# One more piece of weight sums ahead of mixing, two weight chunks rounded at other places, and half of a scaling given to ScalarE

## The chip, the cores and the metric

The kernel runs on one core of a Trainium2 chip. The metric is the device time of one execution in microseconds. The core has five engines with instruction queues of their own: PE (matrix products), DVE (vector), ACT (scalar), POOL (GpSimd) and SP, which only issues transfers. Each runs its queue in order; semaphores tie them together.

## The reference

One decoder block for 512 positions of width 1024, all in float32. Cut to what matters here:

```python
h = rmsnorm(x, norm1_g)
z = h @ w_in + b_in                       # split in five: GLU, two for the recurrence, two gates
u = silu(layernorm(depthwise_conv31(glu(z))))
y_a = u @ conv_w_out + conv_b_out
y_b = (rg_lru(conv4(z_rx)) * gelu(z_rg)) @ lru_w_out
m = sigmoid(z_ga) * y_a + sigmoid(z_gb) * y_b
x = x + m @ w_mix_out                     # "mixing"
h = rmsnorm(x, norm2_g)                   # "norm 2"
x = x + (silu(h @ ffn_w1) * (h @ ffn_w3)) @ ffn_w2     # SwiGLU, width 2816
return rmsnorm(x, norm_f_g)
```

## The kernel before, in words

**Products in split float32.** Every float32 operand is split into a high part, rounded by a copy on ACT (`split_to`, L133: "cast"), and a low part, the difference, by a subtraction on DVE or POOL (L129). A product is three matmuls: high by high, high by low, low by high.

**Weight chunks.** Weights come in chunks of 128 x 1024, listed in the order of use. `emit_chunk` loads one into one of 4 raw buffers and rounds it into one of 5 split buffers (`hl`). `weights(key, ahead)` emits all chunks up to the one asked for and `ahead` more; the default look-ahead is 4. `emit_to(n)` emits chunks up to number n at the place where it stands in the code. At the end of mixing the chunks are, in order: `t2_2` and `t2_3` of mixing, then for SwiGLU `b11_1`, `b21_1`, `b11_2`, `b21_2`, `t4_1`, `t4_2`, `f1_0`, `f3_0`, `f1_1`, `f3_1`, and those for k=3. The profile shows the SwiGLU ones as `hl_fb`, `hl_ft` and `hl_f`. The low parts of `t4_2` and `f1_0` are POOL's, the others DVE's.

**Seven products instead of eight.** Mixing, most of SwiGLU's first two products and its last one use a scheme of two by two blocks in which sums of blocks are multiplied, seven products instead of eight. The sums of the weights' blocks are made by the kernel: a "piece" is two loads of 256 KB, four additions or subtractions, and a store of 512 KB to memory, from where the chunks are read later. `make_f_sums` does most pieces before mixing, one step of it after each matrix product; from step `SUMS_EACH[0]` to `SUMS_EACH[1]` a piece starts at each step, otherwise at every second or third. `OUT_IN` of the pieces for the last product are made there. `mix_end` makes three more, and `out_step` makes the rest during SwiGLU, where `OUT_PIECES` says in which of the steps of block k a piece begins (its loads are issued by POOL, its sums are DVE's). Three buffers hold the pieces (`wsums`).

**The end of mixing and norm 2.** Here the order on PE, ACT and DVE is written out by hand (`manual_schedule`); elsewhere a scheduler orders each engine's queue. `run` takes the last chunk of mixing with `get(kh - 1, ...)` and calls `mix_end`. There `second()` does the last products, six `plus` add them on DVE to four halves of the row tiles 0 and 1 of x (`x` at L940), and `scaled(t, 1)` does the rest of norm 2 for tiles t=0 and 1: the square of the second half on ACT (L561), the root on ACT (L562), the reciprocal on DVE (L563), and the scaling of both halves i=0, 1 into `xs` on DVE (L1100). Then PE does `third` for k=0 and 1, and `turn_half` turns the scaled tiles: for each of 8 columns c, PE transposes tiles 0 and 1 into a PSUM bank (`th`, L579), ACT rounds the high part (`h2<c>h`, L582), DVE makes the low part (`h2<c>l`, L583), after which the bank is free. It is called for c=0 to 3 and c=4 to 7 with six products of `third` behind each, and has four banks to go round. Columns 0 to 3 read half 0 of `xs`, columns 4 to 7 read half 1.

**Behind it** come the first halves of SwiGLU blocks 1 and 2 (`b0.half`, `b1.half`, `fourth`), with the turning of row tiles 2 and 3 between them (`turn`), also by hand and with two banks; then `b.first`, `f_inputs`, and block 0, which is not of the seven-product form and takes the chunks `f1_0`, `f3_0`, `f1_1`, `f3_1`.

Of the kernel before, what the change touches and what calls it, by code (L numbers as in the profile page):

```python
# [10 lines left out]
AF = mybir.ActivationFunctionType  # L11
ALU = mybir.AluOpType
# [22 lines left out]
AHEAD = 4  # L35
# [10 lines left out]
PIECES = 3  # L46


OUT_PIECES = {0: "1", 1: "101", 2: "01", 3: "11", 4: "101", 5: "101", 6: "101", 7: "111", 8: "101", 9: "101", 10: "100"}
SEVEN = (1, 2, 3, 4, 5, 6, 7, 8, 9, 10)  # L50


BEGUN, BEGUN_LATER = (1, 2), (3,)
SUMS_AT, SUMS_STEP, SUMS_LAG, STORE_LAG = 4, 3, 2, 5
SUMS_DENSE, SUMS_OWN, SUMS_EACH = 20, 52, (60, 68)


F_MIX, OUT_MIX, LATE_LAG = 2, 1, 8
OUT_IN = 1

KEPT = {2: 1, 3: 2, 4: 3, 5: 4, 6: 5, 7: 6, 8: 7, 9: 7, 10: 7}

# [34 lines left out]
def tile_block(ctx, tc, a, out):  # L97
# [25 lines left out]
    vec, act, pe, pool_e = nc.vector, nc.scalar, nc.tensor, nc.gpsimd  # L123


    newest = {}
# [19 lines left out]
    emitted = [0]  # L146
# [35 lines left out]
    def emit_to(n):  # L182
        while emitted[0] < min(len(chunks), n):
            emit_chunk()
# [67 lines left out]
    class Quartered:  # L252
# [39 lines left out]
        def get(self, k, *names, ahead=AHEAD):  # L292

            out = []
            for n in names:
                if n in self.parts:
                    out.append(self.parts[n][k])
                    continue
                key, i = self.at[n, k]
                if key not in self.loaded:  # L300
                    self.loaded[key] = weights(key, ahead)
                h, l = self.loaded[key]
                out.append((h[:, i, :], l[:, i, :]))
            return out
# [645 lines left out]
    class Sevenfold:  # L950
# [42 lines left out]
        def run(self, sums, begun, end):  # L993
# [4 lines left out]
            n, kh, get = self.name, self.kh, self.q.get  # L998
# [45 lines left out]
                        plus(2 + i, 1, r5[i])  # L1044

            act.activation(warm, late[-1][1][0][:, :1].bitcast(F32), AF.Sqrt, scale=0.0, bias=eps_t)
            last = get(kh - 1, "b22", "t2", "t3", ahead=AHEAD - 1)
            end(lambda: second(kh - 1, *last), plus, r1, r2, r7, third)

    m7 = Sevenfold(mixq)  # L1050
# [15 lines left out]
    x2 = [[longt(f"x2{t}{h}") for h in range(2)] for t in range(NT)]  # L1066
# [13 lines left out]
    def mix_end(second, plus, r1, r2, r7, third):  # L1080
        made = []

        def store():
            with tc.issue_after(newest["any"]):
                piece_store(*made.pop(0))

        for n in range(F_MIX + OUT_MIX):
            name, halves, dest = mix_todo.pop(0)
            with tc.issue_after(newest["any"]):
                made.append((piece_load(name, halves), dest))  # L1090
            if n < 2:
                piece_sums(*made[-1], pool_e)
        sc = [[longt(f"xs{t}{h}") for h in range(2)] for t in range(NT)]
        xs.extend(sc)
        begun = [rstd_begin(x2[t][0], sc[t][0]) for t in range(2)]

        def scaled(t, h):
            r = rstd_end(begun[t], x2[t][h], sc[t][h])
            for i in range(2):
                newest["scaled"] = vec.tensor_scalar(out=sc[t][i], in0=x2[t][i], scalar1=r, scalar2=None, op0=ALU.mult).ins  # L1100
                nc.sync.dma_start(x2_kept[t][i][:, :], x2[t][i])


        with tc.manual_schedule(engines={ET.PE, ET.Activation, ET.DVE}):
            second()
            plus(0, 1, r1[0])
            plus(0, 1, r2[0])
            plus(2, 1, r1[0])
            plus(1, 1, r1[1])
            plus(1, 1, r2[1])  # L1110
            plus(3, 1, r1[1])
            for t in range(2):
                scaled(t, 1)

            for i in range(2):
                third(i, range(2))
            for q in range(2):
                turn_half("th", xs, "norm2_g", h2p, 0, [bank, bank2], range(4 * q, 4 * q + 4))
                for i in range(2):
                    third(i, [2 + q])  # L1120


            for c in range(ND):
                f_full.append(longt(f"hf{c}"))
                full(f_full[c][:, LO], c, LO)
            with tc.issue_after(newest["full"]):
                piece_sums(*made[2], pool_e)
            for i in range(2):
                plus(2 + i, 1, r7[i])
                plus(2 + i, 0, r7[i])  # L1130
            begun.extend(rstd_begin(x2[t][1], sc[t][1]) for t in (2, 3))
            emit_to(emitted[0] + 1)
            for i in range(2):
                plus(2 + i, 0, r1[i])
            for t in (2, 3):
                scaled(t, 0)
        while made:
            store()

    m7.run(x2, lambda k: None, mix_end)  # L1140


    o7 = Sevenfold(outq, LATE_LAG)
    out_stores, out_n = [], [0]
    out_at, out_steps = [None, None], {k: list(v) for k, v in OUT_PIECES.items()}

# [150 lines left out]
    with tc.manual_schedule(engines={ET.PE, ET.Activation, ET.DVE}):  # L1297
# [20 lines left out]
        for b in (b0, b1):  # L1318
            b.copy()
            b.fourth_end()  # L1320
    with tc.issue_after(turned[0]), tc.issue_after(turned[1]):
        for b in begun.values():
            b.first()
        emit_to(emitted[0] + 4)
        f_inputs()

    for k in range(KF):
# [28 lines left out]
    x2 = [[longt(f"x2b{t}{h}") for h in range(2)] for t in range(NT)]  # L1356
# [99 lines left out]
```

## Time and profile before

| | |
|---|---|
| Median of 3 runs | 799.51 us (798.9 to 799.93) |
| The profiled execution | 798.86 us, span of its instructions 797.0 us |
| PE busy | 786.5 us (99%) |
| DVE busy | 695.8 us (87%) |
| ACT busy | 472.6 us (59%) |
| POOL busy | 360.2 us (45%) |
| Granted TensorE clock | 0.998 |

The profile comes from one execution. In its rows, `out<-in` are the kernel's tiles, `L` is the line of the kernel before, and a bracket says how long the engine was idle before and what ended that. In the rows of stages stand: the stretch in us, its length, busy time and instructions of PE, of its weight loads (PEld), of DVE, ACT and POOL, the clock, the share of the transfer engines, and GB/s. In the rows of time stand start and duration.

### The profile page before, as it was taken

What the parts mean: (1) busy time and instruction counts of PE and PEld (TensorE: products, weight loads), DVE (VectorE), ACT (ScalarE), POOL (GpSimd) and SP (SyncE); (2) the same over time, 40 slices, a digit from 0 to 9 for tenths busy, and PEclk for the clock granted to TensorE, in tenths of its full rate; (3) what the DMA queues carried; (4) which work ended last, traced back from release to release, by engine and by line L of the source; (5) the groups of instructions that cost most, each with busy time, mean ns of one, the idle gap of its engine ahead of it and who ended that gap; (6) DMA issues with size and microseconds to landing.
All of it is one profiled execution on the core that took longest, in us unless ns stands there. A gap on an engine that the chain in (4) does not pass through costs nothing.

```text
span 797.0 us, 12582 instructions
## 1 busy us (share of the span) xinstructions
PE 786.5 (99%) x4374; PEld 688.8 (86%) x4374; DVE 695.8 (87%) x1097; ACT 472.6 (59%) x674; POOL 360.2 (45%) x347
## 2 busy tenths in 40 slices
PE   8999999999999999999999999999999999999996
PEld 7988888888888888888888797999999999888885
DVE  5799999999998997985899868898877798999956
ACT  7446688777679665562326466544455555556843
POOL 2576778788869988853350482113222221000000
PEclk9999999999999999999999999999999999999999
DMA  7746566577776786979987987588998898878652
GB/s 222 190 122 177 157 191 201 174 236 236 195 246 212 249 264 195 295 236 295 296 293 240 275 259 217 157 267 269 343 309 291 297 325 299 235 235 269 197 169 105
DMA packets 181074, 188.13 MB, mean 236 GB/s; under 512 B 14119, under 2 KB 142035, under 8 KB 181011
## 3 DMA queue, kind: packets, MB, share of 16 engines
q1 hardware_dynamic: 172195, 156.66, 63.8%
q0 software_dynamic: 8672, 30.41, 11.2%
q8 instruction: 34, 0.56, 0.3%
q10 hardware_dynamic: 144, 0.26, 0.1%
q14 instruction: 29, 0.24, 0.1%
HBM read 145.48 MB, written 38.80 MB: 231 GB/s over the span
## 4 chain that ended last, share of the span: by engine, by line
PE 95%; DVE 2%; ACT 1%; DMA 0%; issue 0%; SPq 0%; DVEq 0%
PE z L539 35%; PE fr L1211 24%; PE or L991 13%; PE yb L539 7%; PE ya L539 5%; PE mxr L991 4%; PE g L860 3%; PE f L539 2%; PE fr L1255 1%; DMA x<-in_x_dram 0%; DVE x L940 0%; PE z L632 0%; PE th L579 0%; PE tx L590 0%; DVE xs L1100 0%
## 5 line engine op out<-in xcount | busy, mean ns | idle before, releaser
L733 DVE SCALAR_TENSOR_TENSOR cv<-u,par,cv 128x511 f32<-128x511 f32 (+17 forms) x240 | 162.6, 728 | 1.1 <-ACT cv L730 0.9
L129 POOL TENSOR_TENSOR hl_in<-raw_in,hl_in 128x1024 fp32r<-128x1024 f32 x51 | 123.3, 2422 | 64.2 <-ACT hl_in L133 43.4
L129 POOL TENSOR_TENSOR fws<-fws 128x256 f32<-128x256 f32 x120 | 104.7, 875 | 75.1 <-DMA fws<-in_ffn_w_dram 69.5
L398 POOL DMA_DIRECT2D ot<-fwso x21 | 15.3, 731 | 166.1 <-DVE fwso L129 158.8
L1211 PE MATMUL fr<-hs_0h,hl_ft 128*128 128x256 f32 x320 | 59.2, 283 | 0.0
L133 ACT CAST hl_in<-raw_in 128x1024 fp32r<-128x1024 f32 x51 | 53.1, 1043 | 2.2 <-DMA raw_in<-in_w_in_dram 1.0
L129 DVE TENSOR_TENSOR hl_ft<-raw_ft,hl_ft 128x1024 fp32r<-128x1024 f32 x39 | 47.5, 1219 | 4.7 <-ACT hl_ft L133 4.7
L129 DVE TENSOR_TENSOR hl_fb<-raw_fb,hl_fb 128x1024 fp32r<-128x1024 f32 x30 | 36.9, 1231 | 15.9 <-ACT hl_fb L133 15.9
L1211 PEld LDWEIGHTS fr<-hs_0h,hl_ft 128*128 128x128 f32 x320 | 50.6, 192 | 0.0
L133 ACT CAST hl_ft<-raw_ft 128x1024 fp32r<-128x1024 f32 x40 | 41.6, 1047 | 12.4 <-PE fr L1211 9.2
L133 ACT CAST hl_fb<-raw_fb 128x1024 fp32r<-128x1024 f32 x30 | 31.5, 1050 | 24.4 <-PE fr L1211 11.6
L1211 PE MATMUL fr<-hs_0l,hl_ft 128*128 128x256 f32 x160 | 45.3, 283 | 0.0
L539 PE MATMUL z<-h10h,hl_in 128*128 128x512 f32 (+1 forms) x110 | 41.4, 378 | 0.0
L539 PE MATMUL z<-h11h,hl_in 128*128 128x512 f32 (+1 forms) x110 | 41.1, 376 | 0.0
L539 PE MATMUL z<-h17h,hl_in 128*128 128x512 f32 (+1 forms) x110 | 41.1, 376 | 0.0
L539 PE MATMUL z<-h13h,hl_in 128*128 128x512 f32 (+1 forms) x110 | 41.1, 376 | 0.0
L539 PE MATMUL z<-h14h,hl_in 128*128 128x512 f32 (+1 forms) x110 | 41.1, 376 | 0.0
L539 PE MATMUL z<-h15h,hl_in 128*128 128x512 f32 (+1 forms) x110 | 41.1, 376 | 0.0
L539 PE MATMUL z<-h16h,hl_in 128*128 128x512 f32 (+1 forms) x110 | 41.1, 376 | 0.0
L539 PE MATMUL z<-h12h,hl_in 128*128 128x512 f32 (+1 forms) x110 | 41.1, 375 | 0.0
L133 ACT CAST hl_ob<-raw_ob 128x1024 fp32r<-128x1024 f32 (+1 forms) x23 | 23.4, 1016 | 23.9 <-PE or L991 12.1
L394 POOL TENSOR_TENSOR fws<-fws 128x256 f32<-128x256 f32 x40 | 32.5, 813 | 2.8
(962 smaller groups left out, 2639.2 us busy)
## 6 DMA issues: line engine op xcount, KB each, us to landing
raw_in<-in_w_in_dram SPq DMA_DIRECT2D x52, 512.0 KB
fws<-in_ffn_w_dram SPq DMA_DIRECT2D x80, 256.0 KB
raw_ft<-fs SPq DMA_DIRECT2D x34, 512.0 KB
fs<-fws SPq DMA_DIRECT2D x23, 512.0 KB
ot<-fwso POOLq DMA_DIRECT2D x21, 512.0 KB, 5.8
fwso<-in_ffn_w_dram POOLq DMA_DIRECT2D x40, 256.0 KB, 7.3
fs<-fws POOLq DMA_DIRECT2D x17, 512.0 KB, 5.0
raw_ob<-in_ffn_w_dram SPq DMA_DIRECT2D x33, 256.0 KB
```

The source lines that it names most:

```text
L129: return eng.tensor_tensor(out=o, in0=x, in1=y, op=ALU.subtract)
L133: copy(h, full)
L394: eng.tensor_tensor(out=q11, in0=q22, in1=q11, op=ALU.add)
L398: return queue.dma_start(dest, raw.rearrange("p (m n) -> p m n", m=dest.shape[1]))
L539: pe.matmul(ps, l, r, start=i == 0, stop=i == n - 1)
L733: vec.scalar_tensor_tensor(out=acc[c][:, s:], in0=u[c][:, : T - s], scalar=dw(c, s), in1=acc[c][:, s:], op0=ALU.mult, op1=ALU.add)
L860: pe.matmul(ps, l, r, start=k == 0, stop=k == len(mms) - 1)
L991: pe.matmul(banks[i], l_[:, ts], r_, start=start and n == 0, stop=stop and n == 2, skip_group_check=again)
L1211: pe.matmul(ps[:, HALVES[i]], lw[:, c, :], rx_, start=not (again or i or c or m), stop=bool(i and c == 3 and m == 2), skip_group_check=True,)
L1255: pe.matmul(self.r4[:, HALVES[i]], lw, rx_, start=not (i or c or m), stop=bool(i and c == 3 and m == 2), skip_group_check=True)
```

## The change

Four things are edited. `OUT_IN` goes from 1 to 2 and `SUMS_EACH` from (60, 68) to (60, 70), so one more piece is made ahead of mixing, and `OUT_PIECES[7]` begins two pieces instead of three. The last get of mixing looks one chunk less ahead. One chunk is emitted behind `scaled` for tiles 0 and 1, and one ahead of `b.first()`, with 3 instead of 4 behind that. In `scaled`, for tiles 0 and 1, half 1 is scaled by ACT instead of DVE.

```diff
-OUT_PIECES = {0: "1", 1: "101", 2: "01", 3: "11", 4: "101", 5: "101", 6: "101", 7: "111", 8: "101", 9: "101", 10: "100"}
+OUT_PIECES = {0: "1", 1: "101", 2: "01", 3: "11", 4: "101", 5: "101", 6: "101", 7: "101", 8: "101", 9: "101", 10: "100"}
...
-SUMS_DENSE, SUMS_OWN, SUMS_EACH = 20, 52, (60, 68)
+SUMS_DENSE, SUMS_OWN, SUMS_EACH = 20, 52, (60, 70)
...
-OUT_IN = 1
+OUT_IN = 2
...
-            last = get(kh - 1, "b22", "t2", "t3", ahead=AHEAD - 1)
+            last = get(kh - 1, "b22", "t2", "t3", ahead=AHEAD - (1 if self.lag else 2))
             end(lambda: second(kh - 1, *last), plus, r1, r2, r7, third)
...
         def scaled(t, h):
             r = rstd_end(begun[t], x2[t][h], sc[t][h])
             for i in range(2):
-                newest["scaled"] = vec.tensor_scalar(out=sc[t][i], in0=x2[t][i], scalar1=r, scalar2=None, op0=ALU.mult).ins
+                if t < 2 and i:
+
+                    act.activation(sc[t][i], x2[t][i], AF.Copy, scale=r)
+                else:
+                    newest["scaled"] = vec.tensor_scalar(out=sc[t][i], in0=x2[t][i], scalar1=r, scalar2=None, op0=ALU.mult).ins
                 nc.sync.dma_start(x2_kept[t][i][:, :], x2[t][i])
...
             for t in range(2):
                 scaled(t, 1)
+            emit_to(emitted[0] + 1)
 
             for i in range(2):
                 third(i, range(2))
...
     with tc.issue_after(turned[0]), tc.issue_after(turned[1]):
+        emit_to(emitted[0] + 1)
         for b in begun.values():
             b.first()
-        emit_to(emitted[0] + 4)
+        emit_to(emitted[0] + 3)
         f_inputs()
```

In the last gets of mixing, the get for k=2 asks for `t2_2` with the default look-ahead 4, which emits up to `b11_2`; the get for k=3 asks for `t2_3`, one chunk later, with 3 (now 2). The chunk emitted behind `scaled` is `b21_2`; each later place in this stage then emits the chunk after the one that it emitted before, up to `b.first()`.

## The prediction

> **What bounds the kernel now.** I read the page's first part, then the stages, then who keeps PE waiting, then the few microseconds around the edits on each engine.
>
> ```profile
> PE 786.5 (99%) x4374; PEld 688.8 (86%) x4374; DVE 695.8 (87%) x1097; ACT 472.6 (59%) x674; POOL 360.2 (45%) x347
> ```
>
> ```profile
> 440.00:460.00 20.00, 19.42 (x97) 15.98 (x96) 17.15 (x31) 9.20 (x21) 10.58 (x14) 1.00 0.89 273
> 460.00:500.00 40.00, 39.79 (x249) 35.57 (x248) 30.63 (x54) 26.01 (x44) 19.17 (x21) 1.00 0.75 225
> 500.00:600.00 100.00, 100.00 (x832) 99.84 (x831) 83.58 (x138) 51.81 (x71) 20.80 (x30) 1.00 0.84 275
> ```
>
> ```profile
> PE th L579 <- DVE xs L1100: 0.6, 1, 0.6
> ```
>
> PE is the bound: 786.5 of 797.0 us. Its idle time in the stages touched is 0.58 us in 440 to 460 and 0.21 us in 460 to 500; in 500 to 600 there is none. The list of waits names the 0.6: a transpose `th` waits for the scaled row tiles `xs`. A change here can gain only what PE waits, and lose whatever a new wait adds; neither is large beside the 0.2% (1.6 us) that a measurement of this kernel can tell from no change.
>
> The place itself, first DVE, then ACT, then PE (start, duration):
>
> ```profile
> 446.97 1.44 DVE L129 TENSOR_TENSOR hl_fb<-raw_fb,hl_fb 128x1024 fp32r<-128x1024 f32 x1 [1.43 <-ACT hl_fb L133]
> 448.33 4.06 DVE L940 TENSOR_TENSOR x<-mxr,x 128x512 f32<-128x512 f32 x6
> 452.31 0.15 DVE L563 RECIPROCAL stats<-stats 128x1 f32<-128x1 f32 x1
> 453.18 0.96 DVE L1100 TENSOR_SCALAR xs<-x,stats 128x512 f32<-128x512 f32 x1
> 454.06 0.15 DVE L563 RECIPROCAL stats<-stats 128x1 f32<-128x1 f32 x1
> 454.25 0.88 DVE L1100 TENSOR_SCALAR xs<-x,stats 128x512 f32<-128x512 f32 x2
> 455.67 0.48 DVE L583 SCALAR_TENSOR_TENSOR h20l<-th,par,h20h 128x256 fp32r<-128x256 f32 x1 [0.53 <-ACT h20h L582]
> 456.85 0.48 DVE L583 SCALAR_TENSOR_TENSOR h23l<-th,par,h23h 128x256 fp32r<-128x256 f32 x1
> ```
>
> ```profile
> 445.88 1.06 ACT L133 CAST hl_fb<-raw_fb 128x1024 fp32r<-128x1024 f32 x1 [1.67 <-PE mxr L991]
> 449.83 0.63 ACT L561 ACTIVATE xs<-x 128x512 f32<-128x512 f32 x1 [2.90 <-DVE x L940]
> 451.83 0.63 ACT L561 ACTIVATE xs<-x 128x512 f32<-128x512 f32 x1 [0.94 <-DVE x L940]
> 452.58 0.29 ACT L562 ACTIVATE stats<-stats 128x1 f32<-128x1 f32 x1
> 455.16 0.47 ACT L582 ACTIVATE h20h<-th,par 128x256 fp32r<-128x256 f32 x1 [2.28 <-PE th L579]
> 456.24 0.48 ACT L582 ACTIVATE h23h<-th,par 128x256 fp32r<-128x256 f32 x1
> ```
>
> ```profile
> 453.94 0.27 PE L579 MATMUL th<-ident,xs 128*128 128x128 f32 x1
> 454.79 0.98 PE L579 MATMUL th<-ident,xs 128*128 128x128 f32 x7 [0.58 <-DVE xs L1100]
> 455.53 0.48 PE L991 MATMUL mxr<-mxt42h,mxvb2h 128*128 128x512 f32 x1
> 457.00 1.03 PE L579 MATMUL th<-ident,xs 128*128 128x128 f32 x8
> 457.79 0.48 PE L991 MATMUL mxr<-mxt43h,mxvb3h 128*128 128x512 f32 x1
> ```
>
> To be seen: the second transpose needs `xs` of tile 1, half 0, which DVE starts at 454.25; PE stands from 453.94 to 454.79, some 0.74 us more than the 0.10 us that a transpose takes (eight from 457.00 to 457.79). The second group at 457.00 reuses the PSUM banks of the first and so needs `h20l` to `h23l` to have read them; `h20l` ended at 456.15, so here PE did not wait. The other wait is at the first unsplit chunk:
>
> ```profile
> 484.06 0.39 PE L539 MATMUL f<-h20h,hl_f 128*128 128x512 f32 x1
> 484.29 0.39 PE L539 MATMUL f<-h20l,hl_f 128*128 128x512 f32 x1
> 484.79 0.50 PE L539 MATMUL f<-h20h,hl_f 128*128 128x512 f32 x1
> 483.52 3.48 DVE L129 TENSOR_TENSOR hl_f<-raw_f,hl_f 128x1024 fp32r<-128x1024 f32 x3
> 481.35 2.94 ACT L133 CAST hl_f<-raw_f 128x1024 fp32r<-128x1024 f32 x3
> ```
>
> The third product of `f3_0` needs its low part, the first of the three subtractions at 483.52 (1.16 us each). From start to start PE takes 0.50 us there (484.29 to 484.79) where it takes 0.23 for the pair before, and the restarted matmul itself lasts 0.50 against 0.39.
>
> **The change, part by part.**
>
> *The shorter look-ahead at the last chunk of mixing moves nothing.* The get before it (k=2, look-ahead 4) has already emitted up to the chunk that the last get asks for with 3; with 2 it asks for one less. So `b11_2`, the 1.44 us at 446.97, stays ahead of the six adds at 448.33, and 452.31 stays the time of the first reciprocal.
>
> *The scaling on ACT.* The trace has this form (128x512, scale from a column) at another line:
>
> ```profile
> L1392 ACT ACTIVATE of<-of,stats x3: 713/722/726, 777.7 to 792.4; 128x512 f32<-128x512 f32 x3
> ```
>
> 0.72 us on ACT takes the place of 0.96 us (tile 0, while POOL works) and 0.44 (tile 1, half of 0.88) on DVE. But ACT runs in order, and the scaling of tile 0 needs the reciprocal of 452.46; behind it is queued the square of tile 1, which began at 451.83. Consecutive ACT instructions overlap by 0.11 (four `h2*h` of 0.47 start 0.36 apart), so: scaling 452.50 to 453.22; square from 453.11; from its start to the end of its square root 1.04 as now (451.83 to 452.87), hence 454.15; reciprocal and its hand-over 0.2, `xs` of tile 1 from 454.37 (now 454.25). The second transpose comes at 454.91: the old stall is 0.12 longer instead of gone.
>
> The Trainium skill ("ScalarE: Activation LUTs", Rules for kernel authors) puts plain multiplications on VectorE, not ScalarE. Its figures for one column operand (186 + 93 + 0.833 per element) make an estimate of 0.71 us, which the row's 0.72 bears out; the sum would be 0.02 less. The rule speaks against this part, and the 0.12 agrees in direction.
>
> *The chunk `b21_2` behind the scalings.* It now stands on ACT (cast) ahead of `h20h`, and on DVE (subtraction) ahead of `h20l`. Its raw data and its buffer are there (the buffer's last reader is the mixing product before 451). Second scaling 454.37 to 455.09, cast from 454.98 for 1.06 to 456.04, where `h20h` started at 455.16; subtraction from 456.06, 1.16 each as in the three at 483.52: `h20l` starts at 457.22 (now 455.67), the four end 1.66 later, 458.88. PE after its first group (455.65) does six products (1.47) and at 457.1 waits for bank after bank; the last pair of transposes goes at 458.88 and the next products at 459.1 instead of 457.79. **+1.3 us.** Nothing hides this: PE has no other work in its written order, and the SwiGLU products and POOL's sums of `h2` are queued behind it. On SP the load of `t4_1` passes a store of sums and the stores of `x2`, which nothing reads before the SwiGLU stage: 0.
>
> *The two chunks of SwiGLU weights.* `f1_0` takes the place of an earlier cast, and `f3_0` the place of `f1_0`:
>
> ```profile
> 470.47 1.05 ACT L133 CAST hl_f<-raw_f 128x1024 fp32r<-128x1024 f32 x1
> 472.12 0.49 DVE L583 SCALAR_TENSOR_TENSOR h26l<-th,par,h26h 128x256 fp32r<-128x256 f32 x1 [0.99 <-ACT h26h L582]
> 473.06 0.38 PE L579 MATMUL th<-ident,xs 128*128 128x128 f32 x2
> ```
>
> The low part of `f1_0` is POOL's (it passes two sums of `h2` there, which only the inputs of the seven products read, later: 0), that of `f3_0` is DVE's. So a subtraction of 1.16 now follows that cast on DVE, ahead of `h26l`. On the old clock: cast to 471.52, subtraction to 472.71, `h26l` to 473.2, whereas the transposes at 473.06 need its bank: **+0.15**. In return `f3_0` is ready ten microseconds early, and 0.50 - 0.23 + 0.11 at 484.79 goes: **-0.38**. Late next is `f1_1`, one chunk later, itself rounded earlier now. Chunks are one ahead from there; ACT's wait for raw data there holds nobody on PE.
>
> *One more piece ahead of mixing* costs two loads of 256 KB, four subtractions on POOL and a store of 512 KB, about 358 to 370 us, ahead of conv chunks on SP's queue:
>
> ```profile
> 360.00:365.00 5.00, 5.00 (x24) 4.14 (x23) 3.94 (x6) 2.28 (x4) 0.94 (x2) 1.00 0.91 314
> 365.00:370.00 5.00, 5.00 (x24) 4.14 (x23) 2.71 (x5) 1.27 (x2) 0.00 (x0) 1.00 0.80 233
> 370.00:375.00 5.00, 5.00 (x24) 4.14 (x23) 2.45 (x3) 1.05 (x1) 2.00 (x2) 1.00 1.02 328
> ```
>
> ```profile
> fws<-in_ffn_w_dram SPq DMA_DIRECT2D x80, 256.0 KB
> fs<-fws POOLq DMA_DIRECT2D x17, 512.0 KB, 5.0
> ```
>
> ```profile
> 380.02 2.35 DVE L129 TENSOR_TENSOR hl_co<-raw_co,hl_co 128x1024 fp32r<-128x1024 f32 x2
> 375.12 43.52 PE ya L539 x192
> ```
>
> 1 MB at 314 to 328 GB/s is 3.3 us; 1.0 us fits into the idle fifth of 365 to 370, so what follows is up to 2.3 us late. The tightest is the third conv chunk: ready at 381.2, used at 375.12 + 2 x 5.44 = 386.0. It has 4.8 us, so the cost is **0**. In the SwiGLU stage one piece less saves DVE four subtractions, where PE never waits: **0**.
>
> **Sum:** 1.3 + 0.15 - 0.38 = +1.1 us. The profiled execution, 798.86 us (span 797.0), becomes 799.95; the median of the runs shown, 799.51, lies 0.65 above it, and on that scale I predict **800.6**.
>
> Bounds: the scalings as short as the 0.63 of L561 take 0.2 off; a subtraction of 1.44 as at 446.97 puts 0.3 on, `xs` at 0.96 instead of 0.44 (POOL still at its sums) puts 0.5 on; the -0.38 may be 0. Own range: +0.6 to +2.3, 800.1 to 801.8.
>
> **The rivals.** *The intended gain:* the reads of the banks or ACT's queue bind less than the order says, the stall before the second transpose goes (0.74), and `f3_0` is early (0.38): -1.1, 798.4. For it: DVE is 86% busy in 440 to 460 and stands right before PE's wait; against it: ACT waits for the reciprocal with the square behind it. The Trainium skill ("Perfetto Trace Analysis", Optimizing Scalar/DVE Operations) says that offloading from a saturated DVE to Scalar may make sense; by that rule this rival holds.
>
> *Slower, by the extra piece:* if it delays the third conv chunk twice, once in front of its own load and once in front of the mixing sums that ACT casts before it (2 x 3.3 = 6.6 against 4.8), PE stands 1.8 us at 386 and the total is +2.9, 802.4. It decides from 4.8 us of delay on. For it: transfer shares near 1 from 370; against: the idle share just before.
>
> *Nothing happens:* the moved chunk is covered by work I overlooked, 799.5.
>
> **The numbers.** Forecast 0.60, intended gain 0.18, extra piece 0.18, nothing 0.04. Slower by over 0.2% (801.1 up) are the upper third of the forecast, 0.18, and the extra piece, 0.18: 0.36. Faster by over 0.2% is the part of the gain that measures above 1.6 us, 0.05. Within: 0.59. The 8-in-10 range goes from 798.7, inside the gain, to 802.4.
>
> **What would show it.** Right: PE's wait before the second transpose of about 0.6 to 0.8 us again; a second one of 0.5 to 0.6 at the start of the second group and smaller ones in it, on `h20l` to `h23l`; `hl_fb` on ACT between the scaling and `h20h`; no wait on `hl_f` of `f3_0`; third conv chunk ready by 383.5. Wrong: second group of transposes right behind the products, or PE waiting near 386.

## The result, and the profile after

The changed kernel takes 803.22 us (median of 7 runs, 801.74 to 805.49), the kernel before, measured beside it on the same chip, 799.13 us (7 runs, 798.72 to 800.36). The ratio is 1.0049, 95% interval 1.0033 to 1.0065: slower, beyond the 0.2% that can be told from no change, and beyond the top of the predicted range, 802.4. The profiled execution of the changed kernel took 803.22 us, its span is 801.1 us against 797.0.

The list of waits on PE between 420 and 490 us, changed kernel (waiting engine, tile and line, what it waited for: us in all, times, longest). Before, this list had one line, of 0.6 us:

```profile
PE mxr L991 <- DVE x L940: 1.4, 1, 1.4
PE th L579 <- DVE xs L1104: 0.7, 1, 0.7
PE th L579 <- DVE h26l L583: 0.7, 1, 0.7
PE th L579 <- DVE h20l L583: 0.5, 1, 0.5
```

Three of the four lines were forecast, at about their place; the first was not, and it is the longest. The stages of the changed kernel (the columns are those of the stages shown before):

```profile
420.00:440.00 20.00, 18.49 (x81) 14.68 (x81) 19.73 (x34) 12.88 (x19) 0.00 (x0) 1.00 0.75 246
440.00:460.00 20.00, 19.07 (x87) 15.16 (x85) 16.73 (x26) 11.23 (x21) 6.78 (x8) 1.00 1.06 309
460.00:500.00 40.00, 38.98 (x248) 34.86 (x249) 31.04 (x58) 24.91 (x45) 23.68 (x26) 1.00 0.76 221
500.00:600.00 100.00, 100.00 (x815) 99.11 (x814) 84.08 (x138) 50.63 (x71) 18.75 (x28) 1.00 0.79 260
```

The same first stage in the kernel before:

```profile
420.00:440.00 20.00, 20.00 (x89) 16.55 (x89) 19.90 (x32) 13.06 (x19) 0.00 (x0) 1.00 0.79 243
```

In mixing PE was busy for all of 20 us before and for 18.49 after. From 500 us on nothing is lost. To see what each place costs, I follow the same PE instruction through both traces. Mixing's last phase (its first product of `hl_mxt` and `mxeb0h`) starts 0.43 us later, a difference that is there since the transposes of the kernel's input at its start (8.59 against 9.01 us), where nothing was changed. From there on:

| stretch on PE | before, us | after, us | lost |
|---|---|---|---|
| last phase of mixing to the first transpose `th` | 434.80 to 453.94 | 435.23 to 456.42 | **2.05** |
| first `th` to the last mixing products (`mxt43h`) | 453.94 to 457.79 | 456.42 to 461.61 | **1.34** |
| from there to the first product of `f3_0`'s block | 457.79 to 478.49 | 461.61 to 483.23 | **0.92** |
| the low part of `f3_0` (third product) | 0.50 from start to start | 0.23 | **-0.37**: the lag behind the kernel before falls from 4.74 to 4.37 us |

The low part of `f3_0` is ready now; PE, changed kernel:

```profile
483.56 0.39 PE L539 MATMUL f<-h20l,hl_f 128*128 128x512 f32 x1
483.79 0.39 PE L539 MATMUL f<-h20h,hl_f 128*128 128x512 f32 x1
```

The four are 3.9 us, and with the 0.43 at the start 4.4, of the span's 4.1; the rest comes back in small pieces later.

**Mixing, 2.05 us.** DVE in the kernel before: the sum that follows the load of the fourth pair of mixing's blocks, and the first two `x` sums of the last phase (start, duration):

```profile
388.43 0.69 DVE L129 TENSOR_TENSOR mxws<-mxws,mxws 128x512 f32<-128x512 f32 x1 [0.16 <-DMA mxws<-in_w_mix_out_dram]
...
432.91 0.68 DVE L940 TENSOR_TENSOR x<-mxr,x 128x512 f32<-128x512 f32 x1
...
434.11 0.68 DVE L940 TENSOR_TENSOR x<-mxr,x 128x512 f32<-128x512 f32 x1
```

DVE in the changed kernel, the same instructions:

```profile
391.40 0.69 DVE L129 TENSOR_TENSOR mxws<-mxws,mxws 128x512 f32<-128x512 f32 x1 [1.62 <-DMA mxws<-in_w_mix_out_dram]
...
436.06 0.68 DVE L940 TENSOR_TENSOR x<-mxr,x 128x512 f32<-128x512 f32 x1
...
437.26 0.68 DVE L940 TENSOR_TENSOR x<-mxr,x 128x512 f32<-128x512 f32 x1
```

And what PE does then, changed kernel:

```profile
439.19 0.73 PE L991 MATMUL mxr<-hl_mxt,mxvb0h 128*128 128x512 f32 x2 [1.37 <-DVE x L940]
```

The sum behind the load starts 2.97 us late (0.43 of it from the kernel's start), and forty microseconds later the `x` sums are 3.15 us late, past the time at which PE needs its banks back. In between DVE stands idle for 0.6 us (before) and 0.7 us (after) in all: there is nothing in which the delay could disappear. The load itself, on SP, and SP's wait at that line between 340 and 392 us, first before, then after:

```profile
382.15 1.06 SPq L311 DMA_DIRECT2D mxws<-in_w_mix_out_dram  x2
...
SPq L311 <- DMA mxt<-mxws: 0.4, 1, 0.4
```

```profile
384.22 0.81 SPq L311 DMA_DIRECT2D mxws<-in_w_mix_out_dram  x2
...
SPq L311 <- DMA mxt<-mxws: 1.3, 1, 1.3
```

Of the load's 2.07 us, 0.43 are the kernel's start. Such a load waits for a store of the sums before it to land, here 0.9 us longer than before. And the stretch before it is where the extra piece lies; the share of the transfer engines, in the last column but one, changed kernel:

```profile
360.00:365.00 5.00, 5.00 (x24) 4.14 (x23) 3.29 (x5) 1.88 (x3) 1.66 (x3) 1.00 1.06 337
365.00:370.00 5.00, 5.00 (x24) 4.14 (x23) 2.75 (x5) 0.63 (x1) 1.74 (x3) 1.00 0.93 275
```

The idle fifth of 365 to 370 us (0.80 before) is filled as forecast, to 0.93.

**The second transpose, 1.34 us.** PE, then ACT, then DVE, changed kernel:

```profile
457.41 0.98 PE L579 MATMUL th<-ident,xs 128*128 128x128 f32 x7 [0.72 <-DVE xs L1104]
...
460.24 1.61 PE L579 MATMUL th<-ident,xs 128*128 128x128 f32 x8 [0.45 <-DVE h20l L583]
```

```profile
454.98 0.73 ACT L1102 ACTIVATE xs<-x,stats 128x512 f32<-128x512 f32 x1 [1.61 <-DVE stats L563]
455.61 0.61 ACT L561 ACTIVATE xs<-x 128x512 f32<-128x512 f32 x1
...
457.50 1.03 ACT L133 CAST hl_fb<-raw_fb 128x1024 fp32r<-128x1024 f32 x1
458.44 0.47 ACT L582 ACTIVATE h20h<-th,par 128x256 fp32r<-128x256 f32 x1
```

```profile
456.87 0.49 DVE L1104 TENSOR_SCALAR xs<-x,stats 128x512 f32<-128x512 f32 x1
458.57 1.23 DVE L129 TENSOR_TENSOR hl_fb<-raw_fb,hl_fb 128x1024 fp32r<-128x1024 f32 x1 [1.21 <-ACT hl_fb L133]
459.71 0.48 DVE L583 SCALAR_TENSOR_TENSOR h20l<-th,par,h20h 128x256 fp32r<-128x256 f32 x1
```

ACT scales tile 0 first and squares tile 1 behind it; the chunk stands ahead of `h20h` and `h20l`. From `xs` to `h20l` it is 2.84 us (forecast 2.85), and the second group of eight transposes takes 1.37 us from start to start of what follows, held by one low part after the other, where it took 0.79.

**The last transposes, 0.92 us.** PE, DVE and POOL, changed kernel:

```profile
477.73 0.44 PE L579 MATMUL th<-ident,xs 128*128 128x128 f32 x2 [0.68 <-DVE h26l L583]
```

```profile
475.38 1.90 DVE L129 TENSOR_TENSOR hl_f<-raw_f,hl_f 128x1024 fp32r<-128x1024 f32 x1 [0.42 <-ACT hl_f L133]
477.21 0.47 DVE L583 SCALAR_TENSOR_TENSOR h26l<-th,par,h26h 128x256 fp32r<-128x256 f32 x1
```

```profile
473.80 2.41 POOL L129 TENSOR_TENSOR hl_f<-raw_f,hl_f 128x1024 fp32r<-128x1024 f32 x1
```

The subtraction of `f3_0` lasts 1.90 us instead of the 1.16 that three such took before. POOL's subtraction of `f1_0` ends at 476.21, and 1.16 on from there is 477.37; DVE's ended at 477.28.

### The profile page after: what moved, and what is told of

It is laid out like the page before. It is cut to its first block, busy times and chain, and to the rows that moved or that the text cites. A ratio compares the mean times of both kernels' runs of the same rounds, so it can differ in the third digit from the quotient of the medians.

```text
span 801.1 us, 12583 instructions
## 1 busy us (share of the span) xinstructions
PE 787.8 (98%) x4374; PEld 688.8 (86%) x4374; DVE 694.5 (87%) x1091; ACT 473.8 (59%) x676; POOL 361.0 (45%) x349
## 4 chain that ended last, share of the span: by engine, by line
PE 81%; DVE 9%; DMA 4%; ACT 2%; issue 2%; SPq 0%; DVEq 0%; ACTq 0%
PE z L539 35%; PE fr L1216 24%; PE or L991 13%; PE g L860 3%; PE f L539 3%; DMA raw_co<-in_conv_w_out_dram 2%; PE mxr L991 1%; DMA raw_lo<-in_lru_w_out_dram 1%; PE yb L539 1%; DMA mxws<-in_w_mix_out_dram 1%; DVE hl_mxb L129 1%; DVE hl_co L129 1%; DVE x L940 1%; PE fr L1260 1%; DVE mxws L129 1%
## 5 line engine op out<-in xcount | busy, mean ns | idle before, releaser
L129 POOL TENSOR_TENSOR fws<-fws 128x256 f32<-128x256 f32 x120 | 102.1, 853 | 73.7 <-DMA fws<-in_ffn_w_dram 67.6
L394 POOL TENSOR_TENSOR fws<-fws 128x256 f32<-128x256 f32 x40 | 32.4, 811 | 2.8
```

The costliest lines, as they stand in the source:

```text
L129: return eng.tensor_tensor(out=o, in0=x, in1=y, op=ALU.subtract)
L394: eng.tensor_tensor(out=q11, in0=q22, in1=q11, op=ALU.add)
```

## The experiments

All are against the kernel before on the same chip, in interleaved runs. "Phase 2" in the expectations is the last phase of mixing.

### Which part costs what: one part taken away, one part alone

The changed kernel without the extra piece:

```diff
-OUT_IN = 2
+OUT_IN = 1
-SUMS_EACH = (60, 70)
+SUMS_EACH = (60, 68)
-OUT_PIECES[7] = "101"
+OUT_PIECES[7] = "111"
```

> The changed kernel without the extra piece (sums ahead of mixing as before), the rest of the change kept. Theory A (the extra piece makes DVE late through the mixing stage and costs 2.0 us there): no wait of PE on x near 437, th and h26l waits stay: 1.9 us over before. Theory B (the mixing wait is a chance of the one profiled execution, the loss is all at norm 2 and behind it): 3.9 us over before, as the changed kernel.

The kernel before with the extra piece alone (the same three lines the other way):

> The kernel before with the extra piece alone. Theory A: a wait of PE on x at the turn of the two phases of mixing, 1.5 to 2.5 us over before. Theory B: within 0.5 us of before, no such wait.

The changed kernel without the chunk behind the scalings:

```diff
             for t in range(2):
                 scaled(t, 1)
-            emit_to(emitted[0] + 1)
```

> The changed kernel without the chunk emitted behind the scalings, so that each chunk up to b.first is rounded where it was before; the scaling on ACT, f3_0 ahead of b.first and the piece stay. Theory A: mixing 2.0, scaling 0.1 to 0.2, no wait at the second group of transposes nor on h26l, f3_0 -0.4: 1.8 us over before. Rival C (the scaling on ACT alone makes the second group late): the wait on h20l stays, about 3.0 us over.

The kernel before with ACT's scaling alone:

> The kernel before with the scaling of half 1 of tiles 0 and 1 on ACT alone. Theory A: the second transpose 0.1 to 0.2 us later than before, nothing else: 0.1 to 0.3 us over before. Rival (it takes DVE time away and so shortens the stall): 0.4 to 0.7 us under before.

| kernel | median (range), us | before, median | ratio, 95% |
|---|---|---|---|
| changed, no extra piece | 801.69 (800.89 to 804.23) | 799.6 | 1.0026 (1.0015 to 1.0038) |
| before + extra piece | 801.58 (798.97 to 806.11) | 799.6 | 1.0022 (1.0006 to 1.0038) |
| changed, no chunk behind the scalings | 801.26 (799.36 to 803.07) | 799.6 | 1.0013 (1.0001 to 1.0025) |
| before + ACT's scaling | 800.39 (799.15 to 802.52) | 799.6 | 1.0008 (0.9998 to 1.0019) |

PE's waits between 420 and 490 us without the piece, then with the piece alone, then with ACT's scaling alone:

```profile
PE th L579 <- DVE xs L1104: 0.7, 1, 0.7
PE th L579 <- DVE h26l L583: 0.7, 1, 0.7
PE th L579 <- DVE h20l L583: 0.5, 1, 0.5
```

```profile
PE mxr L991 <- DVE x L940: 3.2, 2, 1.8
```

```profile
PE mxr L991 <- DVE x L940: 1.4, 1, 1.4
PE th L579 <- DVE xs L1104: 0.7, 1, 0.7
```

The piece alone costs 2.0 us by the medians and puts the wait in mixing there and no other; its profiled execution, 803.34 us, is 1.8 above its median. Without the piece the time is 2.1 us above the kernel before instead of 4.1, the wait in mixing is gone from the list, and the other three stay, with 1.33 and 0.89 us lost at their places. Without the chunk the wait on `h20l` is gone and 3.97 us pass from first `th` to `mxt43h` instead of 5.19 (3.85 before): of the 1.34 us, 1.22 are the chunk's and 0.12 the scaling's. But the third answer says that the wait in mixing can be there without the piece too, as long as in the changed kernel: 1.85 us are lost at that place in this one execution. So no single profile gives the piece's price; the 2.0 us rest on the medians, once by taking it away and once by adding it. The rival that called the wait a chance of the execution is right in part: it comes and goes in kernels with the piece and without, and by the medians the piece makes it larger, or more frequent, or both.

### How the piece costs: begun earlier, without its sums, over another queue, without its loads

The changed kernel with all pieces begun two steps earlier:

```diff
-SUMS_AT = 4
-SUMS_EACH = (60, 70)
+SUMS_AT = 2
+SUMS_EACH = (60, 68)
```

> The changed kernel with the same number of pieces ahead of mixing, but the pieces begin two steps earlier, so that the extra piece's transfers and POOL sums do not lie on top of the loads for the mixing sums. Theory A (the extra piece's loads bring the fourth pair of mixing sums' loads about 3 us later, DVE works without a gap from 393 to 438, and so the x sums that phase 2 of mixing needs come late): DVE's mxws starts at 388 to 389.5 instead of 391.4, the wait of PE on x at 439 falls from 1.4 to below 0.5, and the time is 1.5 to 2 below the changed kernel, some 2.1 above the kernel before. Rival (the wait on x comes from what the rest of the change does, or is a chance of that execution): the wait stays or falls whatever the start of the pieces, and the time stays where the changed kernel is, 3.5 to 4 above.

The changed kernel without POOL's four sums for the extra piece:

```diff
-                        piece_sums(raw, dest, pool_e)
+                        if at != 69:
+                            piece_sums(raw, dest, pool_e)
```

> The changed kernel whose extra piece has its loads and its store but not its POOL sums (that piece's weight sums are left out). If the transfers delay the mixing sums' loads (theory A): DVE's mxws still starts at about 391, PE still waits 1 us or more on x, and the time is that of the changed kernel, 3.5 to 4 above the kernel before. If POOL's work does it (POOL is held up and with it the transfers that it issues, or DVE is slowed by POOL's reads and writes): the wait on x falls below 0.5, and the time is 2 lower than the changed kernel.

The changed kernel with the extra piece's loads on POOL's queue:

```diff
-                    raw = piece_load(name, halves)
+                    raw = piece_load(name, halves, pool_e if n == 69 else nc.sync)
```

> The changed kernel whose extra piece is loaded over POOL's queue instead of SP's; the bytes are the same. If the extra piece costs by its place in SP's queue (the mixing loads and stores stand behind its two loads there): the mixing loads L311 of the fourth pair are issued near 382.5 after the start instead of 384.2, mxws starts 45.5 us or more ahead of phase 2, PE's wait on x falls below 0.5, and the time is 1.5 to 2 below the changed kernel. If it costs by its bytes, whatever the queue: the wait stays at 1.4 or more and the time at 3.5 to 4 above the kernel before.

The changed kernel without the extra piece's loads:

```diff
-                    raw = piece_load(name, halves)
+                    if n == 69:
+                        raw = wsums.tile([P, 1024], F32, tag="wsum", name=f"fws{name}")
+                        pool_e.memset(raw, 1.0)
+                    else:
+                        raw = piece_load(name, halves)
```

> The changed kernel whose extra piece is not loaded (its buffer is filled by POOL with a constant instead, so that this piece's weight sums are left out); its POOL sums and its store of 512 KB stay. A piece moves 2 loads of 256 KB and one store of 512 KB, 1.0 MB and not the 1.5 MB that two earlier expectations said. If the bytes ahead of the mixing sums' loads are the price: with half of them gone mxws starts about 45 us ahead of phase 2 (43.8 in the changed kernel, 46.4 in the kernel before), PE's wait on x falls to 0.5 or less, and the time is about 1 below the changed kernel, 2.5 to 3 above the kernel before. If the price is the store alone or the shift of all that is issued behind an extra step: as the changed kernel, 3.5 to 4 above the kernel before.

| changed kernel with | median (range), us | before, median | ratio, 95% |
|---|---|---|---|
| pieces begun earlier | 802.45 (801.66 to 808.25) | 799.69 | 1.0057 (1.0033 to 1.0081) |
| no sums on POOL | 803.57 (802.52 to 808.99) | 799.69 | 1.0066 (1.0041 to 1.0090) |
| loads on POOL's queue | 807.04 (806.09 to 808.64) | 799.35 | 1.0096 (1.0079 to 1.0113) |
| no loads | 802.38 (800.61 to 806.08) | 799.38 | 1.0034 (1.0018 to 1.0049) |

Waits on `x` in mixing without POOL's sums, then with the loads on POOL's queue, then without loads:

```profile
PE mxr L992 <- DVE x L941: 2.4, 2, 1.4
```

```profile
PE mxr L991 <- DVE x L940: 3.2, 2, 1.8
```

```profile
PE mxr L995 <- DVE x L944: 1.0, 1, 1.0
```

Whether beginning earlier helps is open. In the profiled execution the wait was 3.0 us in all, where I expected less than 0.5; but that execution took 807.89 us. Four of the seven took 801.7 to 802.5, at a granted clock of 0.999 over the whole execution, the other three 805.4 to 808.3 at 0.993 to 0.995, and the median, 2.8 above the kernel before, is not told apart from the changed kernel's. POOL's sums are not the price: without them the wait stays. Nor is it the place in SP's queue: with two loads less on SP the fourth pair's load was issued at 385.93, later than the 384.22 of the changed kernel, and the kernel is the slowest of all. I expected this to be a gain or nothing. Its profiled execution is 2.9 us longer than that of the changed kernel, and the difference lies in mixing: 5.35 us are lost there instead of 2.05, of which 1.71 is a lower clock (next section). Why the loads come later over this queue was not taken apart. The Trainium skill ("DMA: Bandwidth & Descriptors", Queues, rings and completion order) says that a transfer engine takes turns between the queues it has work for, packet by packet; by that a piece doesn't escape the others by another queue, and the trace agrees as far as that its bytes delay the load from either. Without the loads, half of the bytes, the wait is 1.0 us instead of 1.4, which fits the bytes as the price, but the intervals of the two kernels overlap: it isn't settled between the bytes and the order of all that shifts with a step more.

### More and fewer pieces

The kernel before with two pieces more, and with one piece less, ahead of mixing:

```diff
-OUT_IN = 1          # with SUMS_EACH = (60, 68)
+OUT_IN = 3          # two more: SUMS_EACH = (60, 72), two fewer under SwiGLU
+OUT_IN = 0          # one less: SUMS_EACH = (60, 66), OUT_PIECES[5] = "111"
```

> The kernel before with two more pieces of weight sums ahead of mixing instead of the one more, and nothing else of the change. If each piece's 1.5 MB of transfers brings the mixing sums' last loads later (theory A): mxws starts about 41.5 us ahead of phase 2 (46.4 before, 43.0 with one more piece alone), PE waits on x for 4 to 7 us in all, and the time is 4 to 5 above the kernel before (one more piece alone measured 2.0). Rival (a chance of the execution): as with one more piece, 2 above.

> The kernel before with one piece of weight sums less ahead of mixing and one more under the FFN, and nothing else. Theory A: PE's wait on x is gone in all executions, the kernel before's spread of 798.6 to 802 closes from above, median 0.3 to 0.8 below the kernel before. Rival (chance): no change in median or spread. Rival (a piece under the FFN costs): slower than before by 0.5 or more.

| pieces against the kernel before | median (range), us | before, median | ratio, 95% |
|---|---|---|---|
| one less | 798.78 (798.04 to 801.24) | 799.84 | 0.9979 (0.9965 to 0.9993) |
| one more (from above) | 801.58 (798.97 to 806.11) | 799.6 | 1.0022 (1.0006 to 1.0038) |
| two more | 802.37 (800.24 to 805.30) | 799.84 | 1.0023 (1.0006 to 1.0039) |

The sign follows the number of pieces in both directions, and one less is a gain of about 1 us, which speaks against chance; its spread did not close from above as I expected (801.24). The second extra piece added much less than the first: 4 to 5 us were expected, 2.5 were measured, and by the ratios one and two can't be told apart. No cost showed under SwiGLU for the piece that moved there.

Most of what is lost in mixing goes with one number, and the rest with a second. For each profiled execution I took how long ahead of the last phase of mixing DVE started the fourth pair's `mxws` sum (before: 434.80 - 388.43), and how much longer than the 19.14 us of the kernel before it took from the start of that phase to the first `th`. The last column is the part of it that the granted clock accounts for: the length of that stretch times what its mean clock lacks to 1.

| kernel | sum ahead by, us | lost, us | of it by the clock |
|---|---|---|---|
| two fewer (last section) | 46.78 | 0.06 | 0 |
| one less | 46.71 | -0.09 | 0 |
| before | 46.37 | 0 | 0 |
| squares first (below) | 46.27 | 0.09 | 0 |
| changed, no piece | 45.77 | 0.37 | 0 |
| squares first, again (below) | 45.76 | 0.26 | 0 |
| changed, no chunk | 45.11 | 1.46 | 0 |
| squares first, one less (below) | 44.67 | 1.26 | 0 |
| changed, no loads | 44.50 | 1.26 | 0 |
| changed, `f1_0` on DVE (below) | 44.45 | 2.68 | 0 |
| before + ACT's scaling | 44.43 | 1.85 | 0 |
| changed, `f3_0` later (below) | 43.96 | 2.19 | 0 |
| two more | 43.92 | 3.76 | 1.71 |
| no POOL sums | 43.85 | 2.90 | 0 |
| changed | 43.83 | 2.05 | 0 |
| before + piece | 42.96 | 5.47 | 1.71 |
| begun earlier | 42.34 | 5.09 | 1.71 |
| loads on POOL's queue | 42.04 | 5.35 | 1.71 |

Down to 46 us ahead nothing is lost. Below that, without the clock's part, about 1 us is lost for each microsecond, with single executions up to 1.1 off that line. The kernel before stands a few tenths inside the free side. This is the slack that I had not looked for. Each row is one execution, and the groups overlap: kernels with as many pieces as before lie at 44.43 to 46.37, those with the whole of one more, on SP's queue and begun as in the change, at 42.96 to 45.11.

The clock is a second price of the same wait. With the piece alone, PE waits 1.82 us up to 438.03 us, and 1.37 more up to 440.34; in the second wait the granted clock (third column from the right) falls to half, for 3.4 us:

```profile
438.00:440.00 2.00, 0.93 (x3) 0.48 (x3) 2.00 (x4) 1.64 (x3) 0.00 (x0) 0.97 1.05 385
440.00:442.00 2.00, 1.66 (x4) 1.38 (x5) 2.00 (x4) 0.00 (x0) 0.00 (x0) 0.50 1.13 331
442.00:444.00 2.00, 2.00 (x7) 1.60 (x7) 2.00 (x4) 1.98 (x4) 0.00 (x0) 0.68 1.22 299
```

In four of the traces it falls so, in the wait or right behind it, and each time it costs 1.71 us; in the others, the changed kernel's among them, it stays at 1.00 through this phase. How long PE must wait for it isn't settled: waits of 0.31 and 1.38 us brought it about with two pieces more, 1.07 and 1.37 without POOL's sums did not. The clocks of whole executions fit this: of the 35 of the kernel before beside which "one less" and "two more" ran, the nine at 0.999 took 799.0 to 800.4 us, the seven at 0.996 or less 800.9 to 804.9. Where the clock fell in those isn't known, as they have no trace.

### The subtraction ahead of `h26l`

The changed kernel with that chunk one step later, behind `h26l`:

```diff
         b1.half(bank, lambda: turn(4, 5), ahead=0)
-        emit_to(emitted[0] + 1)
         turn(6, 7)
+        emit_to(emitted[0] + 1)
```

> The changed kernel with one line moved: the chunk of f3_0 that is emitted between the two halves of the second transpose comes behind the step on x of row tiles 6 and 7 (h26l's) instead of ahead of it. Theory 1 (the 0.91 us that PE lost before its last transposes is h26l waiting behind the DVE subtraction hl_f, which ran 1.90 us beside a POOL hl_f of 2.41 us): PE's wait of 0.68 on DVE h26l at about 477.7 goes to 0 to 0.2, hl_f is behind h26l, the third f3_0 product still does not wait, and the time is 0.7 to 0.9 below the changed kernel, some 3.2 above the kernel before. Rival (PE is at that place late for another reason, the transposes' own copies of the half before): the wait stays at 0.5 or more under another name, and the time stays 4 above the kernel before. The waits of 0.72 on xs and 0.45 on h20l stay in both.

The changed kernel with the subtraction of `f1_0` on DVE, so that POOL has none to do beside that of `f3_0`:

```diff
-                wchunk(f"f1_{j}", ..., lo=vec if j else pool_e)
+                wchunk(f"f1_{j}", ..., lo=vec)
```

> The changed kernel whose first f1 chunk is subtracted on DVE, which is idle at that place for 2.5 us, instead of on POOL; f3_0 stays where the change put it. If the 1.90 us of f3_0's subtraction on DVE is the price of POOL's subtraction running beside it: f3_0's takes 1.16 to 1.25, h26l starts 0.7 earlier, PE's wait of 0.68 on h26l goes to 0 to 0.1, and the time is 0.7 to 0.9 below the changed kernel. Rival (the tile itself is slow, or PE and ACT slow it): 1.9 again, and the wait stays.

The first took 803.14 us (800.44 to 806.19; before 799.69; ratio 1.0048, 1.0030 to 1.0066), the second 804.26 us (802.34 to 808.12; before 799.35; ratio 1.0062, 1.0040 to 1.0084). In neither did the time show the 0.7 to 0.9 us that I expected, since mixing's wait varies by more; the traces show it. DVE with the chunk later:

```profile
476.76 0.48 DVE L583 SCALAR_TENSOR_TENSOR h26l<-th,par,h26h 128x256 fp32r<-128x256 f32 x1 [0.99 <-ACT h26h L582]
...
478.06 1.42 DVE L129 TENSOR_TENSOR hl_f<-raw_f,hl_f 128x1024 fp32r<-128x1024 f32 x1 [0.43 <-ACT hl_f L133]
```

There is no wait on `h26l`, and from `mxt43h` to the first product of `f3_0`'s block it is 20.70 us, as before: the 0.92 are gone, and the third product still doesn't wait. With `f1_0` on DVE, first DVE, then POOL:

```profile
472.85 2.69 DVE L129 TENSOR_TENSOR hl_f<-raw_f,hl_f 128x1024 fp32r<-128x1024 f32 x1 [0.64 <-ACT hl_f L133]
...
476.24 1.57 DVE L129 TENSOR_TENSOR hl_f<-raw_f,hl_f 128x1024 fp32r<-128x1024 f32 x1
```

```profile
471.94 2.51 POOL L129 TENSOR_TENSOR hl_ft<-raw_ft,hl_ft 128x1024 fp32r<-128x1024 f32 x1 [1.41 <-ACT hl_ft L133]
476.00 0.73 POOL L1078 TENSOR_TENSOR hf<-h24h,h24l 128x256 f32<-128x256 f32 x1 [1.55 <-DVE h24l L583]
```

The wait on `h26l` is gone, but the moved subtraction met another one of POOL's and took 2.69 us, which makes `h24l` late instead (a wait of 0.2); 0.83 of the 0.92 us stay lost. The cure failed, but the rows bear out the cause: each of these subtractions ends about 1.1 us after the POOL instruction that was running when it started (474.45 to 475.54, 476.73 to 477.81, in the changed kernel 476.21 to 477.28).

### A version that does what was meant, and one that beats both

In the kernel before: the square and root of both tiles first, DVE scales their first halves and ACT, behind both, the second halves; the chunk of `f3_0` one step early, ahead of `b.first()`; no chunk behind the scalings.

```diff
             for t in range(2):
-                scaled(t, 1)
+                rs.append(rstd_end(begun[t], x2[t][1], sc[t][1]))
+                newest["scaled"] = vec.tensor_scalar(out=sc[t][0], in0=x2[t][0], scalar1=rs[t], ...).ins
+            for t in range(2):
+                act.activation(sc[t][1], x2[t][1], AF.Copy, scale=rs[t])
...
+        emit_to(emitted[0] + 1)
         for b in begun.values():
             b.first()
-        emit_to(emitted[0] + 4)
+        emit_to(emitted[0] + 3)
```

> The kernel before with two things alone: on ACT the squares and square roots of the first two row tiles come one after the other with nothing between them and the two scalings of second halves behind both, with DVE scaling the first halves; and the chunk of f3_0 comes one step earlier, ahead of the second transpose. No extra piece, no chunk between scaling and second half. Theory (ACT's scaling costs time only because the second square waits behind it, and what is behind the scalings delays h20l): PE's first wait at the second transpose, 0.97 on xs in the kernel before's pattern, falls by 0.5 to 0.8, the third f3_0 product does not wait (0.37 less), no wait on h20l or h26l, and the time is 0.7 to 1.1 below the kernel before. Rival (the chain through the square root, reciprocal and scaling keeps its length, since DVE's xs of tile 1 now ends the wait): first wait as before, gain 0.4 or less. Mixing's wait on x of 0 to 1.4 varies from execution to execution in both.

The same again, and with one piece less ahead of mixing:

> The same kernel as the one with the squares first and the early chunk of f3_0, beside the one with a piece less. Its first measurement was 0.3 below the kernel before, while its profiled execution, without a wait in mixing, was 0.8 shorter than that of before. Expected again 0.3 to 0.8 below, with executions near 798.3 where mixing does not wait and near 799.7 where it does.

> The run before with the squares first and the chunk of f3_0 early (three terms: no wait at the second transpose, no wait of the third f3_0 product, mixing as in the kernel before), and one piece of weight sums less ahead of mixing than the kernel before (made under the FFN instead). If the stretch of transfers ahead of mixing is what sets DVE's last sums for mixing, one piece less starts that mxws 47 us or more ahead of phase 2 (46.4 in the kernel before, 43.8 in the changed one), PE never waits on x, and the executions lie close together: median 798.2 to 798.6, highest below 799.5. Rival (mixing's wait is a chance that has nothing to do with the pieces): the spread of 2 us stays, median 799.3. Rival (one more piece under the FFN costs there): 799 or more with no wait in mixing.

With two less (one more from ahead of mixing is made during it, `F_MIX, OUT_MIX = 3, 0`, in the place of one that goes under SwiGLU, `OUT_PIECES[6] = "111"`):

> The fastest kernel so far (squares first, chunk of f3_0 early, one piece less ahead of mixing, 1.6 below the kernel before) with one more piece taken from ahead of mixing, one under the FFN more. If the bytes ahead of mixing set the wait on x: mxws starts 47 us ahead of phase 2, no wait on x in the profiled execution, all executions below 799, median 797.9 to 798.2. If the FFN or mixing has no room for it: 798.5 or more, with a wait on DVE or POOL in the FFN that was not there.

| kernel | median (range), us | before, median | ratio, 95% |
|---|---|---|---|
| squares first | 799.39 (798.21 to 800.24) | 799.69 | 0.9994 (0.9985 to 1.0002) |
| the same again | 799.18 (798.16 to 807.30) | 799.84 | 0.9994 (0.9968 to 1.0020) |
| with one piece less | 798.27 (797.84 to 799.86) | 799.84 | **0.9973 (0.9959 to 0.9988)** |
| with two less | 798.15 (797.44 to 799.60) | 799.38 | **0.9984 (0.9972 to 0.9996)** |

PE and ACT with the squares first:

```profile
454.23 1.24 PE L579 MATMUL th<-ident,xs 128*128 128x128 f32 x8
```

```profile
452.88 0.29 ACT L562 ACTIVATE stats<-stats 128x1 f32<-128x1 f32 x1
453.08 1.32 ACT L1117 ACTIVATE xs<-x,stats 128x512 f32<-128x512 f32 x2
```

All eight transposes go in one group of 1.00 us up to the next product, where it took 1.59 before (in the expectation 0.97 stands for the wait of 0.58; it is the duration of the row with it). There is no wait left on PE in this stage. Both scalings stand behind both roots. Whether ACT is needed for it stays open: a version with all four scalings on DVE, first halves first, was not run. The span of this execution is 0.8 us shorter than that of before; two measurements of it can't be told from no change, since mixing's wait comes and goes in it too. With one piece less it is 1.6 us faster than before on the same chip, and some 5.7 us faster than the changed kernel, each taken against its own runs of the kernel before (-1.57 and +4.09). My expectation that mixing would never wait then was wrong: the profiled execution (799.6 us) waits 0.8 us on `x`. With two less the profiled execution waits nowhere in this stage and takes 797.44 us, but executions of 799.6 remain. Which of the two is faster is open; their intervals overlap.

## Why the prediction was wrong, by its steps

The forecast was +1.1 us, "no change" by the bound; measured were +4.1.

- **The extra piece at 0 is the step that failed.** The working had the transfers up to 2.3 us late, and the load was 2.07 us late, 0.43 of it from the kernel's start. It then looked for the tightest use of this among the conv chunks and stopped there. The tightest use stood further behind on the same queue, the fourth pair of loads for mixing's own sums, whose reader, DVE, has only some 0.7 us of idle time in the next forty microseconds. By the medians the piece costs 2.0 us, taken away or alone; in the profiled execution of the changed kernel 2.05 are lost at that place. The rival that named the extra piece had its price nearly right (+2.9 in all) and its place wrong: PE did not stand at 386 us, but at 439. Neither has a term for the granted clock, which took another 1.71 us where the piece was profiled alone.
- **The subtraction ahead of `h26l` at 0.15 is a term of the right mechanism and the wrong size:** 0.92, since 1.16 us became 1.90 beside POOL's subtraction, which the same part of the prediction had placed there and counted as 0.
- **The scaling on ACT** (+0.12) was right: 0.12 and 0.16 by two runs, and the square queued behind the scaling is the reason, as putting it ahead showed.
- **The chunk behind the scalings** (with the scaling +1.3): right, 1.34, and gone when the chunk is taken away.
- **`f3_0` early** (-0.38): right, 0.37. **The shorter look-ahead** moves nothing: `hl_fb` still stands at 449.44, ahead of the six sums at 450.81. **One piece less under SwiGLU**: 0, PE has no idle time from 500 to 600 us after the change either.
- **The Trainium skill's rule ("Perfetto Trace Analysis", Optimizing Scalar/DVE Operations) that offloading from a saturated DVE to Scalar may make sense**, behind the rival of the intended gain, did not hold here with the order as changed; with the squares first the offload came with some 0.6 us less of PE's time.
- **The own range** starts lower than its terms: with the one term that takes something off, 0.2, the sum is +0.9, and nothing named leads down to +0.6.

The sum with these two terms as measured in the profiled execution, 2.05 + 1.34 + 0.92 - 0.37, is 3.9.

## What to carry to other kernels

When a step adds transfers, look first at what is queued next behind them and who reads that, and follow that reader to the next wait that the bound engine has on it: an engine at full load carries a delay on, here for forty microseconds (2.97 us late became 3.15). How much room there is can be read from the trace as the lead of a sum over its use; where the lead is within the spread from execution to execution, cost is a matter of how often. Read the granted clock around a wait of PE before putting a price on it: in four executions here PE's idle time was 45 to 60% of what the wait cost. Ahead of a latency chain through an in-order queue, put all links of the chain first and the work that only uses spare time last.

## What the runs showed of the hardware

A DVE subtraction of two operands in SBUF that starts while POOL runs one does not go slower, it waits: 1.16 us alone became 1.42, 1.57, 1.90 and 2.69, the longer the more of POOL's instruction was left. The sum of `h2` that POOL then starts beside it takes 1.70 to 1.72 us instead of 0.73. The Trainium skill ("SBUF — State Buffer", SBUF: two separate sides) states this as an exclusive lock of the port pair that the two share, held for a whole instruction; the ends of the rows above agree with it within 0.1 us.

The granted TensorE clock of this one core fell to 0.50 in four traces during mixing, in or right behind a wait of PE, for 3.4 us; each time it cost 1.71 us.
